# Down projection of a SwiGLU encoder block: 12 of 22 FFN pairs by seven block products, in two passes over the PSUM banks

## The chip, the cores and the metric

The kernel runs on one core of one Trainium2 chip. The metric is the device time of one execution in microseconds, where lower is better. Before the change three runs took 2675.44, 2680.14 and 2686.07 us, so the median is 2680.14 us.

## The reference

One encoder block is computed on 512 tokens of width 2048 in float32: token mixing (two attention branches, merged and projected), then a SwiGLU feed-forward network of width 5632, each with a residual and a LayerNorm. The change touches the end of the second part alone:

```python
h = modulate(layer_norm(x), shift2, scale2)
f = (jax.nn.silu(h @ w_ffn_gate[l]) * (h @ w_ffn_up[l])) @ w_ffn_down[l]
x = layer_norm_affine(DEEPNORM_ALPHA * x + gate2 * f, ln2_g[l], ln2_b[l])
```

## The kernel before

Every float32 operand of a matmul is split into a high part in the fp32r format and a low part (the remainder): ScalarE casts (line 97), VectorE subtracts (line 98, both inputs in SBUF). One block product is then three matmuls (`mm3`, lines 79 to 81).

The 5632 FFN features are 22 pairs of two 128-feature blocks. For pairs 2 to 21 the gate and up projections already use seven products in place of eight: a unit of work loads 512 KB of weights, `weight_sums` (line 1045) forms four sums of weight blocks on GpSimd (lines 1053 to 1055) and splits raw blocks and sums (ACT and DVE), and TensorE runs 42 matmuls with 256 columns. Four units make one projection of a pair. The hidden state of a pair (silu of gate times up, line 1133) goes to DRAM as one 512 KB transfer (`store_hid`, line 1010).

The down projection is plain. `down` (line 1166) goes over groups of four pairs. For each of four 512-column chunks it takes four PSUM banks (one for each 128-token tile) and for every pair of the group loads 256 rows by 512 columns of weights (512 KB), splits them (one cast, one subtraction of 128x1024) and runs 24 matmuls with 512 columns, as eight block products of a 128-feature block with a 128-token tile. `drain` (line 1150) then multiplies the four banks by the gate row and adds them to the residual in SBUF, on VectorE. Hidden states of the next group come back from DRAM (`load_hid`, line 1100: one transfer, one cast, one subtraction). The last two pairs go token tile by token tile, with weights that GpSimd has multiplied by the gate row (line 1203), so that the final LayerNorm can start early.

Staging: four tiles `raw` of 128x1024 take all loads, four tiles `wh` and four `wl` hold split weights. PSUM has eight banks: four with the tag s, two g, two t. The order of the instructions on each engine is not written by hand: it is fixed when the program is built. Each engine takes its own list in order, and so does each queue of DMA issues (SP issues the weight loads).

## Time and profile before

| what | value |
|---|---|
| median of three runs | 2680.14 us |
| the profiled execution: its own time | 2681.6 us |
| its span | 2679.8 us (1.8 us lie around it) |
| granted TensorE clock, mean | 0.987 of 2.4 GHz |
| busy: PE, DVE, ACT, POOL | 97%, 69%, 39%, 49% of the span |
| gate and up projections by products | about 1390 to 2185 us |
| down projection | about 2185 to 2668 us |

All instructions of one engine run in order, so a share of busy time says little by itself: what matters is whether TensorE finds its operands ready in a stage. A busy time of GpSimd or VectorE contains the time in which an instruction has been started and is held up, so the durations of equal instructions are compared below, the shortest with the longer ones.

### The profile page before, as it was taken

How to read it: one execution, taken by the hardware profiler on the slowest of the kernel's cores; microseconds unless marked ns; L12 is line 12 of the kernel's file. 1: busy time of each engine (PE TensorE's matmuls, PEld its weight loads, DVE VectorE, ACT ScalarE, POOL GpSimd, SP SyncE). 2: the span in 40 equal slices, each digit the busy share in tenths (PEclk: the TensorE clock that was granted, in tenths of full speed). 3: DMA queues.
4: the chain of work that ended last, by engine and by line, in shares of the span. 5: the costliest groups of instructions: out<-in, count | busy, mean ns of one | idle time of the engine just before them, and what ended most of it. 6: DMA issues, size and time to landing. Idle time of an engine off the chain costs nothing.

```text
span 2679.8 us, 40193 instructions
## 1 busy us (share of the span) xinstructions
PE 2601.6 (97%) x15563; PEld 2318.5 (87%) x15563; DVE 1846.5 (69%) x2178; ACT 1053.4 (39%) x1525; POOL 1303.1 (49%) x1093
## 2 busy tenths in 40 slices
PE   5999999999989999999899999999999999999998
...
DVE  8986688774678744577777777677677655445566
ACT  5542334332345533345644444444444432222321
POOL 4638788776764011011358767787776720000023
PEclk8999999999999999999999999999999999999999
...
GB/s 349 298 219 231 174 204 241 244 242 189 213 153 134 122 145 146 225 234 240 231 183 120 117 120 123 113 119 122 115 119 121 116 208 162 110 111 132 151 125 87
DMA packets 330799, 456.11 MB, mean 170 GB/s; under 512 B 19656, under 2 KB 208480, under 8 KB 330096
## 3 DMA queue, kind: packets, MB, share of 16 engines
...
## 4 chain that ended last, share of the span: by engine, by line
PE 46%; POOL 2%; issue 1%; DVE 1%; ACT 0%; POOLq 0%; DVEq 0%
PE ps_s L80 8%; PE ps_s L79 7%; PE ps_s L81 7%; PE ps_g L80 4%; PE ps_g L81 4%; PE ps_g L79 4%; PE ps_t L81 4%; PE ps_t L80 4%; PE ps_t L79 4%; POOL tt L1053 1%; POOL tt L1054 0%; POOL tt L1055 0%; DVE wl L98 0%; ACT wh L97 0%; DVE lr L1051 0%
## 5 line engine op out<-in xcount | busy, mean ns | idle before, releaser
L98 DVE TENSOR_TENSOR wl<-raw,wh 128x1024 fp32r<-128x1024 f32 (+2 forms) x342 | 452.1, 1326 | 328.3 <-ACT wh L97 324.9
L97 ACT CAST wh<-raw 128x1024 fp32r<-128x1024 f32 (+2 forms) x342 | 345.7, 1015 | 657.5 <-PE ps_s L81 262.9
L98 DVE TENSOR_TENSOR wl<-tt,wh 128x1024 fp32r<-128x1024 f32 x160 | 235.7, 1474 | 171.3 <-ACT wh L97 171.1
L1053 POOL TENSOR_TENSOR tt<-raw 128x512 f32<-128x512 f32 x160 | 249.3, 1559 | 184.3 <-DMA raw<-in_w_ffn_gate_dram 61.3
L232 POOL TENSOR_TENSOR acc<-acc,tmp 128x512 f32<-128x512 f32 (+1 forms) x214 | 295.6, 1381 | 74.9 <-ACT tmp L230 62.1
L97 ACT CAST wh<-tt 128x1024 fp32r<-128x1024 f32 x160 | 167.6, 1049 | 307.7 <-PE ps_s L80 136.8
L1051 DVE TENSOR_TENSOR lr<-raw,hr 128x768 fp32r<-128x768 f32 x160 | 217.8, 1362 | 42.6 <-ACT hr L1050 41.7
L1203 POOL TENSOR_TENSOR raw<-raw,gate 128x512 f32<-128x512 f32 x16 | 25.8, 1640 | 400.4 <-DMA raw<-in_w_ffn_down_dram 399.5
L228 POOL TENSOR_SCALAR tmp<-braw,csil 128x512 f32<-128x512 f32 x112 | 140.8, 1259 | 120.8 <-DMA braw<-in_w_ada_dram 117.6
L1050 ACT CAST hr<-raw 128x768 fp32r<-128x768 f32 x160 | 133.6, 835 | 150.8 <-PE ps_s L80 73.1
L1055 POOL TENSOR_TENSOR tt<-raw,tt 128x256 f32<-128x256 f32 x160 | 174.8, 1094 | 11.7
L1054 POOL TENSOR_TENSOR tt<-raw,tt 128x256 f32<-128x256 f32 x160 | 171.6, 1073 | 11.7
L79 PE MATMUL ps_g<-hTh,wh 128*128 128x512 f32 x384 | 153.4, 402 | 0.0
L80 PE MATMUL ps_g<-hTl,wh 128*128 128x512 f32 x384 | 151.2, 394 | 0.0
L81 PE MATMUL ps_g<-hTh,wl 128*128 128x512 f32 x384 | 151.2, 394 | 0.0
L222 DVE SCALAR_TENSOR_TENSOR acc<-braw,csil,acc 128x512 f32<-128x512 f32 x112 | 111.9, 1000 | 47.7 <-DMA braw<-in_w_ada_dram 46.8
L79 PE MATMUL ps_s<-wh,hTh 128*128 128x512 f32 (+1 forms) x384 | 138.1, 361 | 0.0
L80 PE MATMUL ps_s<-wl,hTh 128*128 128x512 f32 (+1 forms) x384 | 137.5, 358 | 0.0
L81 PE MATMUL ps_s<-sh,wl 128*128 128x256 f32 x480 | 135.9, 284 | 1.4 <-DVE wl L98 1.4
L81 PE MATMUL ps_s<-wh,hTl 128*128 128x512 f32 (+1 forms) x384 | 137.2, 358 | 0.0
L79 PE MATMUL ps_s<-sh,wh 128*128 128x256 f32 x480 | 135.1, 282 | 2.0 <-ACT wh L97 2.0
L80 PE MATMUL ps_s<-sl,wh 128*128 128x256 f32 x480 | 136.1, 284 | 0.0
...
## 6 DMA issues: line engine op xcount, KB each, us to landing
braw<-in_w_ada_dram SPq DMA_DIRECT2D x128, 512.0 KB, 4.2
...
```

The lines of the kernel that those rows point to most:

```text
L79: nc.tensor.matmul(ps, lhsT=ah, rhs=bh, start=start, stop=False)
L80: nc.tensor.matmul(ps, lhsT=ah, rhs=bl, start=False, stop=False)
L81: nc.tensor.matmul(ps, lhsT=al, rhs=bh, start=False, stop=stop)
L97: nc.scalar.copy(out=h[:, :n], in_=src)
L98: nc.vector.tensor_tensor(out=l[:, :n], in0=src, in1=h[:, :n], op=ALU.subtract)
L228: nc.gpsimd.tensor_scalar(out=dst[:, :n], in0=v[:, k, :], scalar1=col, scalar2=1.0, op0=ALU.mult, op1=ALU.mult)
L232: nc.gpsimd.tensor_tensor(out=acc2[:, :n], in0=acc2[:, :n], in1=dst[:, :n], op=ALU.add)
L1050: nc.scalar.copy(out=hr, in_=b[:, :, 1:4, :])
L1051: nc.vector.tensor_tensor(out=lr, in0=b[:, :, 1:4, :], in1=hr, op=ALU.subtract)
L1053: nc.gpsimd.tensor_tensor(out=t[:, :, 0:2, :], in0=b[:, :, 0:1, :].broadcast_to([P, 2, 2, P]), in1=b[:, :, 1:3, :], op=ALU.subtract)
L1054: nc.gpsimd.tensor_tensor(out=t[:, :, 2, :], in0=b[:, :, 2, :], in1=t[:, :, 0, :], op=ALU.subtract)
L1055: nc.gpsimd.tensor_tensor(out=t[:, :, 3, :], in0=b[:, :, 3, :], in1=t[:, :, 2, :], op=ALU.subtract)
```

## The change

For the 12 pairs 2 to 13 the down projection uses seven products in place of eight. The blocks of a pair are its two 128-feature blocks, two halves of the tokens and two halves of the output columns. Three of the products need one set of sums of hidden blocks and weight blocks, four need another, so that the 12 pairs are gone through twice (first pass, second pass), each time for both 1024-column halves c = 0 and c = 1 (in two 512-column pieces). The banks collect over all 12 pairs: six banks in the first pass, eight in the second.

- `hidden_sums` forms four sums of 128x256 on GpSimd when a pair of gate and up is done, and stores 7 blocks with six transfers from ACT's queue in place of one.
- `load_set` brings a set of hidden blocks back (three blocks for the first pass, four for the second), with a cast and a subtraction, into one of 12 ring tiles. Four of them (D) take the place of the pool of the gate and up stage.
- `weights1` (first pass, one unit of 18 matmuls): two transfers (512 and 256 KB), two subtractions of 128x512 on GpSimd, and two splits (1024 and 512 columns). `weights2` (second pass, one unit of 24 matmuls): four transfers of 256 KB, one subtraction of 128x1024 on GpSimd and one of 128x512 on VectorE, and two splits of 1024.
- `half_tile` alternates the four `raw` tiles with four new tiles `tp`, which lie in the pool on the right side, where the token sums sh and sl of the gate and up stage lay.
- The products' sums are collected in the x3 tiles, without the gate row. `convert` multiplies them by the gate row on GpSimd (128x1024) and adds the scaled residual on VectorE, four times for each half.
- The other eight pairs go through the plain `down` as before (now without the first-group case), the last two as before.

```diff
+    GROUPS = [[2, 3, 4, 5, 6, 7, 8, 9, 10, 11, 12, 13]]
+    PLAIN = [[0, 1, 14, 15], [16, 17, 18, 19]]
+    N_LAST = 2
+    by_sums = [g for grp in GROUPS for g in grp]
+    RING = [(a_pool, "Ah0"), (a_pool, "Al0"), (a_pool, "Ah1"), (a_pool, "Al1"),
+            (m0, "Mh0"), (m0, "Ml0"), (m0, "Mh1"), (m0, "Ml1")]
...
+    def half_tile():
+        place[1] += 1
+        if extra_tiles and place[1] % 2:
+            return extra_tiles[0].tile([P, 1024], F32, tag="tp", name="tp", bufs=4)
+        return raw_tile()
...
+    def load_set(arr, g, n):
+
+        v = half_tile()[:, :n * 256].rearrange("p (b n) -> p b n", b=n)
+        nc.sync.dma_start(out=v, in_=arr[g])
+        tl = ring_tile((n, g))
+        nc.scalar.copy(out=tl[:, 0:n, 0:256], in_=v)
+        nc.vector.tensor_tensor(out=tl[:, 0:n, 256:512], in0=v, in1=tl[:, 0:n, 0:256], op=ALU.subtract)
+        return tl
...
+    def hidden_sums(g, eg, e):
+
+        nc.gpsimd.tensor_tensor(out=e[:, 0], in0=eg[:, 1], in1=eg[:, 2], op=ALU.add)
+        nc.gpsimd.tensor_tensor(out=e[:, 1], in0=e[:, 0], in1=eg[:, 3], op=ALU.subtract)
+        nc.gpsimd.tensor_tensor(out=e[:, 2], in0=eg[:, 1], in1=eg[:, 3], op=ALU.subtract)
+        nc.gpsimd.tensor_tensor(out=e[:, 3], in0=eg[:, 0], in1=e[:, 1], op=ALU.subtract)
+        nc.scalar.dma_start(out=set1_d[g][:, 0:2, :], in_=e[:, 0:2])
+        nc.scalar.dma_start(out=set1_d[g][:, 2, :], in_=eg[:, 3])
+        for b, (t, k) in enumerate(((eg, 0), (e, 2), (eg, 2), (e, 3))):
+            nc.scalar.dma_start(out=set2_d[g][:, b, :], in_=t[:, k])
...
-        store_hid(g, eg)
...
+        if g in by_sums:
+            hidden_sums(g, eg, eu)
+        else:
+            store_hid(g, eg)
...
+    dr = push("dr", "left")
+    vacant += range(len(RING), len(RING) + 4)
+    RING += [(dr, f"D{i}") for i in range(4)]
...
+    def weights1(g, c):
+        a, b = half_tile(), half_tile()
+        av, bv = a.rearrange("p (b n) -> p b n", b=2), b[:, :512]
+        nc.sync.dma_start(out=av, in_=w_rows(g, 0, c))
+        nc.sync.dma_start(out=bv, in_=w_rows(g, 1, c)[:, 1, :])
+        nc.gpsimd.tensor_tensor(out=av[:, 1], in0=av[:, 1], in1=av[:, 0], op=ALU.subtract)
+        nc.gpsimd.tensor_tensor(out=bv, in0=bv, in1=av[:, 1], op=ALU.subtract)
+        ah, al = split(a, 1024)
+        bh, bl = split(bv, 512)
+        return ((2, (ah[:, :512], al[:, :512])), (1, (bh[:, :512], bl[:, :512])), (0, (ah[:, 512:], al[:, 512:])))
+
+    def weights2(g, c):
+        a, b = half_tile(), half_tile()
+        av, bv = a.rearrange("p (b n) -> p b n", b=2), b.rearrange("p (b n) -> p b n", b=2)
+        for j in range(2):
+            nc.sync.dma_start(out=av[:, j], in_=w_rows(g, 1, c)[:, 1 - j, :])
+            nc.sync.dma_start(out=bv[:, j], in_=w_rows(g, 0, c)[:, 1 - j, :])
+        nc.gpsimd.tensor_tensor(out=bv, in0=bv, in1=av, op=ALU.subtract)
+        nc.vector.tensor_tensor(out=bv[:, 1], in0=bv[:, 0], in1=bv[:, 1], op=ALU.subtract)
+        ah, al = split(a, 1024)
+        bh, bl = split(b, 1024)
+        return ((3, (ah[:, :512], al[:, :512])), (0, (ah[:, 512:], al[:, 512:])), (1, (bh[:, :512], bl[:, :512])),
+                (2, (bh[:, 512:], bl[:, 512:])))
...
+    def products(pairs, sets, weights, c, step):
+        bk = None
+        for u, g in enumerate(pairs):
+            ws = weights(g, c)
+            if bk is None:
+                bk = [dbank() for _ in range(2 * len(ws))]
+            step(u, False)
+            for j, (b, w) in enumerate(ws):
+                for i in range(2):
+                    mm3(bk[2 * j + i], block(sets[g], b, i), w, u == 0, u == len(pairs) - 1)
+            step(u, True)
...
+    def convert(c, ts=range(NT)):
+        for t in ts:
+            zv = quad(x2[t], c)
+            xc = half_tile().rearrange("p (b n) -> p b n", b=2)
+            nc.sync.dma_start(out=xc, in_=quad(x2_d[t], c))
+            nc.gpsimd.tensor_tensor(out=zv, in0=zv, in1=quad(gate2, c), op=ALU.mult)
+            nc.vector.scalar_tensor_tensor(out=zv, in0=xc, scalar=ALPHA, in1=zv, op0=ALU.mult, op1=ALU.add)
...
+                    vacate((3, pairs[u]))
+                if done:
+                    tick((lambda g=pairs[u]: need2(g)) if c == 1 else None)
+            bk = products(pairs, set1, weights1, c, step)
...
+        for c in range(2):
+            def step(u, done):
+                if done and c == 1:
+                    vacate((4, pairs[u]))
+                if done:
+                    tick(following.pop(0) if following and c == 1 else None)
+                if done and c == 1 and final and u % 2 and u // 2 < NT:
+                    convert(0, [u // 2])
+            bk = products(pairs, set2, weights2, c, step)
+            for i in range(2):
+                add(nc.vector, z(0, 1, i, c), bk[i])
+            for i in range(2):
+                add(nc.vector, z(0, 0, i, c), bk[2 + i])
+            for i in range(2):
+                add(nc.vector, z(1, 0, i, c), bk[4 + i])
+                add(nc.vector, z(1, 1, i, c), bk[4 + i])
+            for i in range(2):
+                add(nc.vector, z(1, 0, i, c), bk[6 + i])
...
+    if PLAIN:
+        convert(1)
+        for grp in PLAIN:
+            queue = down(grp, (0, 2, 1, 3), queue)
```

How the order of the instructions moves, at three places (names carry a buffer's number; the rows of the changed kernel have its own line numbers, some 190 lines further down at the end).

First VectorE. Before, in the first group of the down projection: the subtraction of the last gate and up pair, then for each unit one split of 128x1024 (line 98), and drains.

```order
L1133 TENSOR_TENSOR eg_21845<-eg_21845,eu_22324 128x1024
L98 TENSOR_TENSOR wl_22450<-raw_22447,wh_22449 128x1024
L98 TENSOR_TENSOR wl_22496<-raw_22493,wh_22495 128x1024
L98 TENSOR_TENSOR wl_22526<-raw_22523,wh_22525 128x1024
L98 TENSOR_TENSOR wl_22556<-raw_22553,wh_22555 128x1024
L1153 TENSOR_TENSOR dtmp_22477<-ps_s_22348,gate2_22347 128x512
L1153 TENSOR_TENSOR dtmp_22480<-ps_s_22349,gate2_22347 128x512
L1156 SCALAR_TENSOR_TENSOR x3_0_22340<-x3_0_22340,dtmp_22477 128x512
L1156 SCALAR_TENSOR_TENSOR x3_1_22341<-x3_1_22341,dtmp_22480 128x512
L1153 TENSOR_TENSOR dtmp_22483<-ps_s_22350,gate2_22347 128x512
L1153 TENSOR_TENSOR dtmp_22486<-ps_s_22351,gate2_22347 128x512
L1156 SCALAR_TENSOR_TENSOR x3_2_22342<-x3_2_22342,dtmp_22483 128x512
```

Now, in the second half (c = 1) of the second pass, each unit has three rows: line 1212 (the weight difference) and two of line 98. Between them stand line 1333 (a plain pair's hidden state) and line 1254 (`convert`).

```order
L1333 TENSOR_TENSOR Al1_24177<-tp_24175,Al1_24177 128x1024
L98 TENSOR_TENSOR wl_24144<-tp_24135,wh_24143 128x1024
L98 TENSOR_TENSOR wl_24148<-raw_24136,wh_24147 128x1024
L1254 SCALAR_TENSOR_TENSOR x3_3_22452<-tp_24225,x3_3_22452 128x2x512
L1333 TENSOR_TENSOR Mh0_24222<-raw_24220,Mh0_24222 128x1024
L1212 TENSOR_TENSOR tp_24181<-tp_24181 128x512
L98 TENSOR_TENSOR wl_24189<-raw_24180,wh_24188 128x1024
L98 TENSOR_TENSOR wl_24193<-tp_24181,wh_24192 128x1024
L1212 TENSOR_TENSOR tp_24230<-tp_24230 128x512
L1333 TENSOR_TENSOR Ml0_24271<-raw_24269,Ml0_24271 128x1024
L98 TENSOR_TENSOR wl_24238<-raw_24229,wh_24237 128x1024
L98 TENSOR_TENSOR wl_24242<-tp_24230,wh_24241 128x1024
```

One row for a unit has become three to five, all with both inputs in SBUF. In the whole pass half, nine rows of line 1333 and four of line 1254 stand ahead of the last unit's split. In the first pass it is seven loads of three blocks (line 1126) for c = 0 and nine of four blocks for c = 1, and three more stand in c = 0 of the second pass.

Second GpSimd. Before, from the end of gate and up (lines 1053 to 1055) its next rows are those of the last two pairs, line 1203:

```order
L1055 TENSOR_TENSOR tt_22208<-raw_22202,tt_22208 128x2x128
L1053 TENSOR_TENSOR tt_22268<-raw_22262 128x2x256
L1054 TENSOR_TENSOR tt_22268<-raw_22262,tt_22268 128x2x128
L1055 TENSOR_TENSOR tt_22268<-raw_22262,tt_22268 128x2x128
L1203 TENSOR_TENSOR raw_24776<-raw_24776,gate2_22347 128x512 x2
L1203 TENSOR_TENSOR raw_24784<-raw_24784,gate2_22347 128x512 x2
```

Now the first pass stands there with two rows for each unit, here at the turn from c = 0 to c = 1:

```order
L1199 TENSOR_TENSOR tp_22904<-tp_22904 128x512
L1200 TENSOR_TENSOR raw_22905<-raw_22905,tp_22904 128x512
L1199 TENSOR_TENSOR tp_22942<-tp_22942 128x512
L1200 TENSOR_TENSOR raw_22943<-raw_22943,tp_22942 128x512
L1199 TENSOR_TENSOR tp_22974<-tp_22974 128x512
L1200 TENSOR_TENSOR raw_22975<-raw_22975,tp_22974 128x512
L1199 TENSOR_TENSOR tp_23006<-tp_23006 128x512
L1200 TENSOR_TENSOR raw_23007<-raw_23007,tp_23006 128x512
```

GpSimd, which had no row in 20 pairs of the down projection, has 24 x 2 rows of 128x512 and 24 of 128x1024 there, and eight of `convert`, four of them after the fourth unit of the second pass's last half.

Third SP's queue at the turn from gate and up to down, with what each issue waits for. Now (tp is the new staging tile, set_d the stored sets):

```order
L1197 DMA raw<-in_w_ffn_down_dram 128x2x512 [waits DMAHW6_49,DVE_49]
L1123 DMA raw<-set_d 128x768 [waits DMAHW3_49,DVE_49]
L1198 DMA raw<-in_w_ffn_down_dram 128x512 [waits DMAHW7_49,DVE_49,Pool_49]
L1197 DMA raw<-in_w_ffn_down_dram 128x2x512 [waits DMAHW4_49,DMAHW0_49,DVE_49]
L1123 DMA raw<-set_d 128x768 [waits DMAHW2_49,DVE_49]
L1198 DMA raw<-in_w_ffn_down_dram 128x512 [waits DMAHW5_49,DVE_49]
L1198 DMA tp<-in_w_ffn_down_dram 128x512 [waits PE_49]
L1197 DMA tp<-in_w_ffn_down_dram 128x2x512 [waits DMAHW1_49]
```

Before, all issues of this place wrote `raw` and waited for its readers alone:

```order
L1103 DMA raw<-hid_d 128x1024 [waits DMAHW7_49,DVE_49]
L91 DMA raw<-in_w_ffn_down_dram 128x2x512 [waits DMAHW2_49,DVE_49]
L91 DMA raw<-in_w_ffn_down_dram 128x2x512 [waits DMAHW3_49,DVE_49,Pool_49]
L91 DMA raw<-in_w_ffn_down_dram 128x2x512 [waits DMAHW4_49,DMAHW0_49,DVE_49]
L91 DMA raw<-in_w_ffn_down_dram 128x2x512 [waits DMAHW5_49,DVE_49]
```

The first issue into `tp` (the second weight block of the first unit) waits for TensorE, which reads sh and sl until the end of the last gate and up pair, and all later issues stand behind it.

## Rows read from the trace of the kernel before

**Rows 1.** It is the profile's first page: the span and the busy time of each engine, and the span in 40 equal slices with the busy tenths of PE, DVE, ACT and POOL and the granted TensorE clock in tenths.

```profile
span 2679.8 us, 40193 instructions
...
PE 2601.6 (97%) x15563; PEld 2318.5 (87%) x15563; DVE 1846.5 (69%) x2178; ACT 1053.4 (39%) x1525; POOL 1303.1 (49%) x1093
...
PE   5999999999989999999899999999999999999998
...
DVE  8986688774678744577777777677677655445566
ACT  5542334332345533345644444444444432222321
POOL 4638788776764011011358767787776720000023
PEclk8999999999999999999999999999999999999999
```

**Rows 2.** It is the busy time by stretch: start and end, length, then busy us and instructions of PE, PEld, DVE, ACT and POOL, the granted clock (1.00 is 2.4 GHz), the busy share of the DMA engines and GB/s. The first three stretches lie in the gate and up projections (the third is the most crowded one there), the last two in the down projection (2190 to 2212 is its start).

```profile
1420.00:2100.00 680.00, 679.11 (x5667) 678.88 (x5666) 488.73 (x425) 282.19 (x323) 510.91 (x412) 1.00 0.37 119
1440.00:1480.00 40.00, 39.11 (x326) 38.88 (x325) 30.05 (x27) 17.66 (x21) 37.02 (x28) 1.00 0.42 132
1500.00:1700.00 200.00, 200.00 (x1671) 200.00 (x1671) 144.01 (x126) 83.42 (x95) 143.21 (x120) 1.00 0.38 119
2190.00:2212.00 22.00, 22.00 (x99) 18.20 (x98) 7.33 (x9) 4.26 (x5) 0.00 (x0) 1.00 0.94 317
2190.00:2640.00 450.00, 450.00 (x1987) 372.73 (x1986) 238.97 (x288) 108.57 (x112) 26.64 (x18) 1.00 0.42 136
```

**Rows 3.** It is the view of one tile, tt (the gate and up weight sums), from 1500 to 2100 us: count, then minimum, median and maximum duration in ns.

```profile
L1054 POOL TENSOR_TENSOR tt<-raw,tt x120: 733/742/1607, 1499.7 to 2099.6; 128x256 f32<-128x256 f32 x120
L97 ACT CAST wh<-tt x120: 1047/1048/1058, 1500.4 to 2099.4; 128x1024 fp32r<-128x1024 f32 x120
...
L98 DVE TENSOR_TENSOR wl<-tt,wh x119: 1214/1505/1934, 1501.5 to 2095.4; 128x1024 fp32r<-128x1024 f32 x119
L1053 POOL TENSOR_TENSOR tt<-raw x119: 1274/1405/2093, 1504.1 to 2097.5; 128x512 f32<-128x512 f32 x119
```

**Rows 4.** It is the same view of the tile lr (the low part of raw gate and up blocks), from 1500 to 2100 us.

```profile
L1051 DVE TENSOR_TENSOR lr<-raw,hr x120: 943/1015/2095, 1498.4 to 2097.4; 128x768 fp32r<-128x768 f32 x120
```

**Rows 5.** It is the same view of the tile raw (where weights and hidden states land) in the down projection, from 2190 to 2680 us, with the DMA issues of SP (SPq) and, in the last row, the time from issue to landing.

```profile
L91 SPq DMA_DIRECT2D raw<-in_w_ffn_down_dram x82: 367/368/384, 2189.9 to 2596.0; - x82
L97 ACT CAST wh<-raw x77: 1044/1055/1057, 2192.0 to 2603.5; 128x1024 fp32r<-128x1024 f32 x77
L98 DVE TENSOR_TENSOR wl<-raw,wh x77: 1212/1224/2208, 2193.6 to 2607.5; 128x1024 fp32r<-128x1024 f32 x77
...
L1203 POOL TENSOR_TENSOR raw<-raw,gate x16: 1287/1474/2279, 2532.4 to 2601.5; 128x512 f32<-128x512 f32 x16
...
L1205 ACT CAST Ah<-raw x8: 621/622/627, 2533.8 to 2559.1; 128x512 fp32r<-128x512 f32 x8
L1206 DVE TENSOR_TENSOR Al<-raw,Ah x8: 674/903/1579, 2534.4 to 2560.7; 128x512 fp32r<-128x512 f32 x8
...
DMA to landing us min/median/max: 3.6/3.7/5.7
```

**Rows 6.** It is VectorE in order of time, from 1632 to 1640 us: start in us, duration in us, engine, line, operation, out<-in and shapes, and in brackets idle time before it.

```profile
1632.71 1.75 DVE L98 TENSOR_TENSOR wl<-tt,wh 128x1024 fp32r<-128x1024 f32 x1
1634.39 1.49 DVE L1051 TENSOR_TENSOR lr<-raw,hr 128x768 fp32r<-128x768 f32 x1
```

**Rows 7.** It is GpSimd over the same time, with the same columns.

```profile
1631.79 1.59 POOL L1054 TENSOR_TENSOR tt<-raw,tt 128x256 f32<-128x256 f32 x1
1633.46 1.60 POOL L1055 TENSOR_TENSOR tt<-raw,tt 128x256 f32<-128x256 f32 x1
1635.03 2.01 POOL L1053 TENSOR_TENSOR tt<-raw 128x512 f32<-128x512 f32 x1
```

**Rows 8.** It is the instructions of GpSimd by line from 1440 to 1480 us: count, busy us, mean ns, and idle time before them.

```profile
L1054 POOL TENSOR_TENSOR tt<-raw,tt 128x256 f32<-128x256 f32 x10 | 14.3, 1433 | 0.6
L1055 POOL TENSOR_TENSOR tt<-raw,tt 128x256 f32<-128x256 f32 x10 | 12.2, 1230 | 0.6
L1053 POOL TENSOR_TENSOR tt<-raw 128x512 f32<-128x512 f32 x8 | 12.0, 1498 | 1.7 <-DVE wl L98 1.7
```

**Rows 9.** It is the same for VectorE from 1440 to 1480 us.

```profile
L98 DVE TENSOR_TENSOR wl<-tt,wh 128x1024 fp32r<-128x1024 f32 x9 | 13.1, 1455 | 11.3 <-ACT wh L97 11.2
L1051 DVE TENSOR_TENSOR lr<-raw,hr 128x768 fp32r<-128x768 f32 x9 | 11.8, 1311 | 0.0
L1133 DVE TENSOR_TENSOR eg<-eg,eu 128x1024 f32<-128x1024 f32 x1 | 1.8, 1765 | 0.0
...
L1085 DVE TENSOR_TENSOR eg<-ps_s,eg 128x512 f32<-128x512 f32 x1 | 0.7, 691 | 0.0
```

**Rows 10.** It is VectorE by line in the down projection, from 2190 to 2480 us.

```profile
L1158 DVE TENSOR_TENSOR x<-x,dtmp 128x512 f32<-128x512 f32 x36 | 23.3, 685 | 0.0
L1153 DVE TENSOR_TENSOR dtmp<-ps_s,gate 128x512 f32<-128x512 f32 x28 | 18.2, 684 | 0.4
L1156 DVE SCALAR_TENSOR_TENSOR x<-x,dtmp 128x512 f32<-128x512 f32 x16 | 10.4, 686 | 0.0
```

243 lines of the change are left out of this document (155 added, 88 removed).

## The prediction

> **What bounds the kernel now.** I read the first page first: TensorE is busy 97% of the span, at full clock in all but the first slice [rows 1]. A busy TensorE may still run at a poor pace, so the second view is the stretches [rows 2]. In the down projection 1987 matmuls of 512 columns start in 450 us: 450 / 1987 = 226.5 ns each, and TensorE is never idle. In gate and up it is 680 / 5667 = 120 ns for 256 columns, with 0.9 us lost in 680. So TensorE bounds both stages, and a matmul taken away is worth its pace, as long as what feeds TensorE keeps up.
>
> The third view is what feeds it. In gate and up GpSimd is busy 511 and VectorE 489 of 680 us [rows 2], but equal instructions of theirs differ by up to a factor of two: GpSimd's 128x256 takes 0.73 to 1.61 us, its 128x512 1.27 to 2.09, VectorE's subtraction of 128x1024 1.21 to 1.93, that of 128x768 0.94 to 2.10 [rows 3, 4]. In the down projection, where GpSimd is idle, that subtraction has a median of 1.22 [rows 5]. The two time lines say why [rows 6, 7]. GpSimd's 128x256 ends at 1633.38; VectorE's subtraction, begun at 1632.71, ends 1.08 later, at 1634.46. GpSimd's next, begun at 1633.46, ends 0.60 after that, at 1635.06; VectorE's 128x768, begun at 1634.39, ends 0.82 after that; and GpSimd's 128x512 ends 1.16 after that. While one runs, the other stands still. I call 1.08, 0.82, 1.16 and 0.60 us the holds of these shapes. The ban holds for VectorE operations with two SBUF inputs: one that reads a bank keeps its 0.69 us in the most crowded stretch [rows 9].
>
> How tightly can holds be packed? From 1440 to 1480 us GpSimd ran 8 of 128x512 and 20 of 128x256, VectorE 10 of 1024 columns and 9 of 768 [rows 8, 9]: 8 x 1.16 + 20 x 0.60 + 10 x 1.08 + 9 x 0.82 = 39.5 us, some 37.5 without an operation cut at either end, so 0.94 to 0.99 of 40, and there TensorE lost 0.9 us [rows 2]. Over 1500 to 1700 (120 GpSimd operations, five pairs of 40 us) it is 40 x (1.16 + 2 x 0.60) + 40 x (1.08 + 0.82) + 5 x 1.08 = 176 us of 200, 0.88, and TensorE lost nothing [rows 2]. I take 0.95 as the limit.
>
> The Trainium skill has this as a rule that speaks against the change (SBUF — State Buffer, Who interferes with whom): a VectorE instruction with two SBUF inputs and a GpSimd instruction that reads SBUF exclude each other for the whole instruction. The trace agrees that one stands still, but not on the whole length: after the other's end 1.08 us are left of an instruction that takes 1.21 alone, and 1.16 of 1.27. Counted by whole instructions (1.22, 0.94 and 0.68 us on VectorE, 1.27 and 2.35 on GpSimd) the four half passes would lose 52 us in place of 38.5 as an estimate, and the sum would be 2708.
>
> **What is taken away.** Each of 12 pairs loses 96 - 84 = 12 matmuls, 144 in all, and TensorE's list is shorter by just that: 144 x 0.2265 = **-32.6 us**. The Trainium skill (TensorE: Matmul & The Clock Gate, Back-to-back issue gap) gives 216 ns for an isolated matmul of 512 columns and 131 in a sustained stream with weight loads. As estimates, by the one the gain would be 31.1 us, by the other 18.9. The 226.5 ns measured here decide against both, so neither gets a chance of its own.
>
> **What is added in the down projection.** A unit of the first pass has 18 matmuls, 4.08 us of TensorE; one of the second 24, 5.44. Two holds have no row. For GpSimd's 128x1024 I go on from 0.60 and 1.16 in a line: 1.16 + 2 x 0.56 = 2.28; its bounds are 1.16 (no dearer than 512 columns) and 2.32 (twice that). For VectorE's 128x512, 0.82 - 0.26 = 0.56, between 0 and its unblocked 0.68 [rows 10]. `convert`'s VectorE operation of 1024 columns I take as a subtraction, 1.08, since the two kinds cost the same 0.68 to 0.69 at 512 [rows 10]. Then one unit holds
>
> - first pass: 2 x 1.16 + 1.08 + 0.56 = 3.96 us;
> - second pass: 2.28 + 0.56 + 2 x 1.08 = 5.00 us.
>
> The loads come on top. By half passes (12 units each):
>
> - first, c = 0: 47.5 + 7 x 0.82 = 53.3, less 3.4 done before the stage (1.16 + 1.08 + 1.16 for what fits into `raw`) = 49.9; at 0.95 52.5 against 48.9 us of TensorE: +3.6.
> - first, c = 1: 47.5 + 9 x 1.08 = 57.2; 60.3 against 48.9: +11.3.
> - second, c = 0: 60.0 + 3 x 1.08 = 63.2; 66.6 against 65.2: +1.3.
> - second, c = 1: 60.0 + 9 x 1.08 + 4 x (2.28 + 1.08) = 83.2; 87.5 against 65.2: +22.3.
>
> Together **+38.5 us**. Split weights are two units ahead at most (four `wh`, two to a unit), so little can be saved up from one half to the next. Packed without any gap it is 1.0 + 8.3 + 0 + 18.0 = 27.3; packed to 0.88, 7.8 + 16.1 + 6.6 + 29.3 = 59.8.
>
> **The turn from gate and up.** The first load into `tp` waits for TensorE's last sh and sl product, and SP's queue, all weight loads, stands behind it. What follows is one issue and landing 0.37 + 3.7, GpSimd 1.16, a cast 0.62, a subtraction 0.68: 6.5 us [rows 5]. TensorE meanwhile has the 12 matmuls of the unit's other block, 2.7 us. I take **+4**, between 0 (the pool lets go earlier) and 6.5.
>
> **Smaller terms.** In gate and up `hidden_sums` adds 4 x 0.60 = 2.4 us of holds to a pair of 336 x 0.12 = 40.3: 0.88 becomes 0.94, just under the limit. VectorE's queue is not blocked by it, since the sums stand some units later in GpSimd's list than their input. I take 0.25 us for a pair, **+3**; bounds 0, and (0.94 / 0.92 - 1) x 40.3 = 0.9 for each, 10. The six stores instead of one are issued by ACT, 39% busy [rows 1]. Draining the banks costs VectorE 4, 4, 10 and 10 bank reads of 0.68 [rows 10]; they ban nothing, and the banks that are needed first were finished half a unit earlier. I take **+2** for the turns, between 0 and 7 (one turn's ten reads). Bringing in the residual (`convert`, c = 1), plain pairs and the last pairs run where VectorE is busy 239 of 450 us [rows 2]: nothing; without that cover four conversions cost 4 x 3.36 = 13. Clock: full throughout the stage before; gaps of 1 to 2 us in a unit could lower it, but then TensorE is waiting anyway.
>
> **Sum:** -32.6 + 38.5 + 4 + 3 + 2 = +14.9 on the profiled execution's 2681.6, so 2696.5. That execution is 1.5 above the median of the runs (2680.1), so I give **2695**. A measurement of this kernel can tell about 0.5% (13.4 us) from no change: the forecast lies just beyond.
>
> **Rivals.**
>
> 1. *Packed holds, no change.* The holds of both engines follow each other without a gap, since both have work queued. Then 27.3 in place of 38.5, 2 for the turn and nothing else: -32.6 + 27.3 + 2 = -3, **2677**. For it: the stretch with 0.94 to 0.99 [rows 8, 9]. Against it: that stretch is short, and a VectorE operation that follows its own kind takes 1.22, not 1.08 [rows 5].
> 2. *The holds fit under TensorE, faster.* If GpSimd's subtraction of whole rows held much less than the gate and up sums do, every unit would be ready in time: -32.6 + 4 + 2 = -27, **2654**. Its place is the first pass with c = 1. It decides when 24 GpSimd operations and VectorE's 12 x 1.64 + 9.7 = 29.4 us fit into 0.95 x 48.9 = 46.5: from 0.71 us for 512 columns downward. For it: no row has the large plain shape. Against it: the plain 128x512 of line 1203 takes at least 1.29 unblocked, as line 1053 does (1.27) [rows 3, 5].
> 3. *The staging tiles, slower still.* With a load a unit of the first pass takes three of eight tiles. A tile's round is 0.37 + 3.7 landing, 2 x 1.16 GpSimd, 1.06 cast, 1.22 subtraction [rows 5], and one hold of waiting on each side, 2.2: 10.9 us. At 8 / 3 = 2.7 units that is 4.1 us a unit, no more than TensorE's own. But 1.31 MB in a unit of 5.0 us is 262 GB/s, where 317 kept the DMA engines 94% busy [rows 2]. If landing takes twice as long, the round is 14.6 us, 5.5 a unit, 0.5 more on 16 units, and late data opens gaps between holds: with packing at 0.90, 55.4 + 63.6 + 70.2 + 92.4 - 228.2 = 53.4, the sum becomes -32.6 + 53.4 + 4 + 3 + 2 + 8 = +38, **2718**.
>
> **How the numbers follow.** Forecast case 0.48, packed holds 0.22, fitting holds 0.14, staging tiles 0.16. The forecast case spreads over packing 0.92 to 0.97, some 2684 to 2712, with two fifths of it within 0.5%. So slower by over 0.5%: 0.58 x 0.48 + 0.16 = 0.44; within 0.5%: 0.22 + 0.20 less 0.02 for the low end of rival 1 = 0.40; faster: 0.14 + 0.02 = 0.16. The range, 2662 to 2726, takes in packing without gaps and at 0.88 with the other terms as chosen (-32.6 + 59.8 + 9 = +36) and a part of the bounds of the smaller terms; it leaves out most of rival 2 and the upper end of rival 3, under 0.2.
>
> **What would show it.** TensorE starts exactly 144 fewer matmuls, still at 226 ns where fed. The first pass with c = 1 lasts about 60 us and the last half of the second about 87, with VectorE and GpSimd together in use without a break and their equal shapes longer than alone; the second pass with c = 0 about 66. GpSimd's 128x1024 takes at least 2.3 us unblocked. At the turn TensorE stands for some 4 us. In the plain pairs nothing is lost. I am wrong if the four half passes take about 228 us (rival 2), if GpSimd's shape is far from 2.3, or if TensorE waits mainly for landings.

## The result and the profile after

The changed kernel takes 2709.4 us (median of four runs, 2707.6 to 2720.7), the kernel before 2678.3 (four runs): ratio 1.012, 95% interval 1.0101 to 1.014. So it is slower by some 31 us. All differences of whole kernels here are under 2%; one is called slower or faster where the interval of its ratio leaves out 1. The forecast was 2695, about 15 slower. The profiled execution takes 2710.6 us with a span of 2708.8, 29.0 longer than that of before.

The first page of the changed kernel, as [rows 1]:

```profile
span 2708.8 us, 40614 instructions
...
PE 2587.2 (96%) x15419; PEld 2292.5 (85%) x15419; DVE 1964.6 (73%) x2194; ACT 1101.0 (41%) x1585; POOL 1556.7 (57%) x1213
...
PE   6999999999989999999899999999999989888998
...
POOL 4638778776744011031279998899767658555003
```

TensorE starts 15563 - 15419 = 144 fewer matmuls, as promised, and is yet less busy in a longer span: slices 33 and 35 to 37 show gaps where before there were none. The second view is the busy time by stretch, with the columns of [rows 2]. The first six stretches go from the first matmul of a half pass to the first of the next: first pass c = 0 and 1, second pass c = 0 and 1, first and second group of plain pairs. Then come a short piece at the turn, and the start of the pairs with sums in gate and up.

```profile
2189.35:2253.31 63.96, 53.84 (x218) 40.52 (x217) 56.46 (x37) 26.43 (x34) 47.69 (x27) 0.95 0.75 245
2253.31:2308.72 55.41, 51.53 (x217) 39.76 (x216) 55.41 (x38) 30.93 (x37) 42.10 (x22) 1.00 0.82 266
2308.72:2384.99 76.27, 68.40 (x289) 54.50 (x288) 55.60 (x48) 31.17 (x33) 38.64 (x14) 0.98 0.61 200
2384.99:2467.60 82.61, 69.31 (x288) 53.12 (x289) 74.95 (x56) 30.01 (x31) 40.19 (x14) 1.00 0.70 230
2467.60:2567.03 99.43, 91.61 (x385) 74.80 (x384) 70.67 (x65) 24.74 (x24) 31.05 (x11) 0.95 0.41 132
2567.03:2654.07 87.04, 87.04 (x385) 72.07 (x384) 42.46 (x51) 16.77 (x16) 2.41 (x1) 1.00 0.27 85
2198.00:2201.00 3.00, 2.95 (x7) 1.80 (x8) 0.71 (x2) 1.32 (x2) 2.54 (x3) 0.50 1.01 344
1420.00:1480.00 60.00, 56.60 (x466) 55.79 (x465) 43.16 (x37) 22.73 (x28) 53.62 (x45) 1.00 0.41 128
```

At 0.2265 us for each of 216, 216, 288, 288 and 384 matmuls TensorE needs 48.9, 48.9, 65.2, 65.2 and 87.0 us. So 15.0, 6.5, 11.0, 17.4 and **12.4** us were lost in the first five stretches, 62.4 together; the second plain group lost nothing. From the first matmul of the down projection to the last of the kernel it is 508.0 us, before 478.5: -32.6 + 62.4 = +29.8, measured +29.5. Gate and up took 3.2 us more, and everything ahead of it 3.7 less in this execution (the 7000th matmul starts at 1411.8 us, before at 1415.5), which makes the 29.0 of the spans.

What TensorE waited for says the same by cause. It is the view of waits (instruction waiting, what released it, us in all, times, longest), for the first pass with c = 0 (two rows), the second with c = 0 (three) and with c = 1 (four), and the first plain group (two):

```profile
PE ps_s L79 <- ACT wh L97: 5.5, 1, 5.5
PE ps_s L80 <- DVE wl L98: 4.5, 7, 1.2
...
PE ps_g L80 <- DVE wl L98: 3.4, 2, 2.7
PE ps_s L79 <- DVE x L1282: 2.2, 1, 2.2
...
PE ps_g L79 <- DVE x L1246: 1.0, 1, 1.0
...
PE ps_g L80 <- DVE wl L98: 7.8, 7, 1.9
PE ps_s L80 <- DVE wl L98: 2.7, 2, 1.5
PE ps_s L79 <- DVE x L1246: 1.9, 2, 1.6
PE ps_g L79 <- DVE x L1246: 1.7, 2, 1.0
...
PE ps_g L80 <- DVE wl L98: 4.1, 1, 4.1
PE ps_g L79 <- DVE x L1246: 3.7, 1, 3.7
```

VectorE's low part (line 98) ends most waits of the passes. Two kinds of wait are larger than forecast: one of 5.5 us for the very first weights, and those for VectorE's drains of a bank (lines 1246 and 1282). Two rows of the views of one tile bear on the terms: the landing of the issues into tp from 2185 to 2200 us, and GpSimd's 128x1024 (minimum, median and maximum in ns).

```profile
DMA to landing us min/median/max: 6.0/7.3/8.5
```

```profile
L1211 POOL TENSOR_TENSOR raw<-raw,tp x16: 2399/2927/3489, 2307.3 to 2451.1; 128x1024 f32<-128x1024 f32 x16
```

The first is far from the 3.7 us of [rows 5]; the second is 2.40 where nothing holds it up.

In the plain group TensorE waits twice. The first wait (3.7 us, to 2472.86) is for a drain. Ahead of it in VectorE's list stands the hidden state of a plain pair (line 1333), and VectorE is idle until ScalarE has cast that, which waits for its landing (the issue is at 2461.93, 7.0 us before the cast). The time lines show it (start, duration, then as in [rows 6]):

```profile
2470.03 2.17 DVE L1333 TENSOR_TENSOR D<-raw,D 128x1024 fp32r<-128x1024 f32 x1 [5.01 <-ACT D L1332]
2472.12 0.68 DVE L1246 TENSOR_TENSOR x<-ps_g,x 128x512 f32<-128x512 f32 x1
...
2468.95 1.05 ACT L1332 CAST D<-raw 128x1024 fp32r<-128x1024 f32 x1 [5.79 <-DMA raw<-hid_d]
```

So this wait is for a landing, passed on by the order of VectorE's list, and no hold. What stood ahead of the second wait (4.1 us, to 2494.80) is seen in VectorE's and GpSimd's time lines from 2480 us:

```profile
2479.80 1.63 DVE L98 TENSOR_TENSOR wl<-raw,wh 128x1024 fp32r<-128x1024 f32 x1
2481.35 3.41 DVE L1254 SCALAR_TENSOR_TENSOR x<-raw,x 128x1024 f32<-128x1024 f32 x1
2484.68 0.68 DVE L1246 TENSOR_TENSOR x<-ps_s,x 128x512 f32<-128x512 f32 x1
2485.28 2.83 DVE L1254 SCALAR_TENSOR_TENSOR x<-tp,x 128x1024 f32<-128x1024 f32 x1
2488.04 3.43 DVE L1254 SCALAR_TENSOR_TENSOR x<-raw,x 128x1024 f32<-128x1024 f32 x1
2491.39 6.67 DVE L98 TENSOR_TENSOR wl<-raw,wh 128x1024 fp32r<-128x1024 f32 x2
```

```profile
2480.31 3.37 POOL L1362 TENSOR_TENSOR tp<-tp,gate 128x1024 f32<-128x1024 f32 x1
2483.63 3.40 POOL L1253 TENSOR_TENSOR x<-x,gate 128x1024 f32<-128x1024 f32 x1
2486.99 3.40 POOL L1362 TENSOR_TENSOR raw<-raw,gate 128x1024 f32<-128x1024 f32 x1
2490.35 3.32 POOL L1253 TENSOR_TENSOR x<-x,gate 128x1024 f32<-128x1024 f32 x1
```

Here the two engines go strictly by turns. Read as in the prediction, from the end of the other engine's operation to its own end, VectorE's 1024 columns hold for 1.08 us (from 2483.68 to 2484.76) and GpSimd's for 2.2 to 2.3 (to 2487.03). GpSimd's operations start 3.3 to 3.4 us apart, VectorE's take 2.8 to 3.4 us in place of 1.21, and the weights that TensorE needs next (line 98, from 2491.39) stand behind three conversions (line 1254).

### The profile page after: what moved, and what is told of

The parts are those of the page before. It is cut to its first block, busy times and chain, and to the rows that moved or that the text cites. A ratio compares the mean times of both kernels' runs of the same rounds, so it can differ in the third digit from the quotient of the medians.

```text
span 2708.8 us, 40614 instructions
## 1 busy us (share of the span) xinstructions
PE 2587.2 (96%) x15419; PEld 2292.5 (85%) x15419; DVE 1964.6 (73%) x2194; ACT 1101.0 (41%) x1585; POOL 1556.7 (57%) x1213
## 5 line engine op out<-in xcount | busy, mean ns | idle before, releaser
L98 DVE TENSOR_TENSOR wl<-raw,wh 128x1024 fp32r<-128x1024 f32 (+2 forms) x342 | 490.1, 1438 | 230.4 <-ACT wh L97 228.9
L97 ACT CAST wh<-raw 128x1024 fp32r<-128x1024 f32 (+2 forms) x342 | 339.3, 995 | 584.2 <-PE ps_s L81 238.6
L98 DVE TENSOR_TENSOR wl<-tt,wh 128x1024 fp32r<-128x1024 f32 x160 | 227.1, 1422 | 191.4 <-ACT wh L97 187.8
L1055 POOL TENSOR_TENSOR tt<-raw 128x512 f32<-128x512 f32 x160 | 239.2, 1496 | 106.7 <-DMA raw<-in_w_ffn_up_dram 53.7
L1053 DVE TENSOR_TENSOR lr<-raw,hr 128x768 fp32r<-128x768 f32 x160 | 211.4, 1322 | 42.2 <-ACT hr L1052 41.5
L1056 POOL TENSOR_TENSOR tt<-raw,tt 128x256 f32<-128x256 f32 x160 | 202.7, 1268 | 10.7
L230 POOL TENSOR_SCALAR tmp<-braw,csil 128x512 f32<-128x512 f32 x112 | 133.9, 1198 | 118.9 <-DMA braw<-in_w_ada_dram 115.5
L1057 POOL TENSOR_TENSOR tt<-raw,tt 128x256 f32<-128x256 f32 x160 | 192.5, 1204 | 11.6
L80 PE MATMUL ps_g<-sl,wh 128*128 128x256 f32 x480 | 135.8, 283 | 0.0
```

The costliest lines, as they stand in the source:

```text
L80: nc.tensor.matmul(ps, lhsT=ah, rhs=bl, start=False, stop=False)
L97: nc.scalar.copy(out=h[:, :n], in_=src)
L98: nc.vector.tensor_tensor(out=l[:, :n], in0=src, in1=h[:, :n], op=ALU.subtract)
L230: nc.gpsimd.tensor_scalar(out=dst[:, :n], in0=v[:, k, :], scalar1=col, scalar2=1.0, op0=ALU.mult, op1=ALU.mult)
L1053: nc.vector.tensor_tensor(out=lr, in0=b[:, :, 1:4, :], in1=hr, op=ALU.subtract)
L1055: nc.gpsimd.tensor_tensor(out=t[:, :, 0:2, :], in0=b[:, :, 0:1, :].broadcast_to([P, 2, 2, P]), in1=b[:, :, 1:3, :], op=ALU.subtract)
```

## Experiments

The theory is the prediction's: VectorE's operations with two SBUF inputs and GpSimd's exclude each other, and the sum of their holds paces the half passes. Its rivals are late transfers, and VectorE's own list (its length, or the order in it). For each kernel the half passes are read off stretches as above, with the same columns.

Each stretch comes from one execution, and kernels whose edits do not touch it show how far it scatters. In the changed kernel, spread, conv_vec and plain_vec the first pass takes 61.4 to 64.7 us with c = 0 and 54.8 to 58.6 with c = 1, the second with c = 0 76.3 to 80.1. In the changed kernel, gate_late and turn_raw the second with c = 1 takes 81.4 to 82.6, and in these three, no_sub and vec_sub the first plain group takes 98.0 to 99.6. A smaller difference than that shows nothing.

**no_sub**: without GpSimd's three subtractions of weights, so that the weight sums are left out.

```diff
-        nc.gpsimd.tensor_tensor(out=av[:, 1], in0=av[:, 1], in1=av[:, 0], op=ALU.subtract)
-        nc.gpsimd.tensor_tensor(out=bv, in0=bv, in1=av[:, 1], op=ALU.subtract)
...
-        nc.gpsimd.tensor_tensor(out=bv, in0=bv, in1=av, op=ALU.subtract)
```

> The changed kernel without the three GpSimd subtractions of weights1 and weights2 (the weight sums are left out; transfers, casts, VectorE's subtractions and all matmuls stay). Holds theory: what TensorE lost in the four half passes beside the turn and the drains (about 6 us in the first pass with c = 0, 6.5 with c = 1, 3 and 13 in the second) comes back, since GpSimd then works there only on the four conversions: the first pass with c = 1 falls from 55.4 us to 49 or 50, the second with c = 1 from 82.6 to about 69, the whole from 2709 to about 2680 (2674 to 2686). Landing theory (late transfers and staging tiles): the same transfers through the same tiles, so the half passes stay within 2 us each and the time stays at 2705 to 2712.

Measured: 2679.2 us, as the holds theory expected, ratio to the kernel before 1.0003 (0.9994 to 1.0012). The four half passes and the first plain group:

```profile
2186.30:2243.03 56.73, 51.04 (x218) 41.43 (x217) 33.59 (x39) 25.89 (x35) 0.00 (x0) 0.94 0.82 277
2243.03:2292.27 49.24, 49.24 (x217) 40.50 (x216) 36.09 (x40) 30.21 (x36) 0.00 (x0) 1.00 0.85 283
2292.27:2361.84 69.57, 67.43 (x290) 54.97 (x288) 41.27 (x45) 30.36 (x32) 0.00 (x0) 0.98 0.66 219
2361.84:2434.80 72.96, 68.66 (x288) 54.48 (x289) 61.16 (x56) 31.83 (x32) 14.51 (x6) 0.98 0.79 274
2434.80:2532.78 97.98, 90.05 (x385) 73.40 (x384) 70.95 (x65) 23.86 (x24) 29.23 (x10) 0.97 0.41 129
```

The first pass with c = 1 is fed without a gap (49.24), though its transfers come at 283 GB/s in place of 266. The four half passes are 29.7 us shorter with the same transfers through the same tiles: the landing theory falls. The second with c = 1 comes to 73.0, where about 69 was expected. VectorE's busy time in that half pass falls from 55.4 to 36.1 us though it lost no operation: the difference was standing still. The plain group's loss stays (98.0 us).

**vec_sub**: the three subtractions on VectorE, in those lines; the last of the three is shown.

```diff
-        nc.gpsimd.tensor_tensor(out=bv, in0=bv, in1=av, op=ALU.subtract)
+        nc.vector.tensor_tensor(out=bv, in0=bv, in1=av, op=ALU.subtract)
```

> The same three subtractions, moved from GpSimd to VectorE. Holds theory: VectorE's 512-column subtraction takes 0.59 us from start to start, its 1024-column one 1.13, in place of GpSimd's holds of 1.16 and 2.24. One unit of the first pass is then 3 x 0.59 + 1.13 = 2.9 us of VectorE against 4.08 of TensorE, of the second 0.59 + 3 x 1.13 = 4.0 against 5.44; with loads of 1.13 a unit 4.0 and 5.1, still under TensorE. The first pass with c = 1 takes 49 to 51 us (55.4), the second with c = 1 loses only what the conversions and drains cost, 72 to 75 us (82.6); whole 2681 to 2688. Landing theory: no change, 2705 to 2712. Third theory, that VectorE's own list is the limit (busy 100% of the first pass with c = 1 already): the added work makes it slower, 2715 or more.

Measured: 2685.7 us, as expected, ratio 1.0024 (1.0014 to 1.0035). The first pass, the second with c = 1 and the first plain group:

```profile
2188.99:2247.83 58.84, 52.26 (x218) 41.82 (x217) 50.29 (x67) 27.20 (x35) 0.00 (x0) 0.94 0.83 272
2247.83:2297.81 49.98, 49.34 (x218) 40.47 (x216) 47.26 (x57) 29.11 (x36) 0.00 (x0) 1.00 0.87 291
2366.24:2443.84 77.60, 70.79 (x289) 55.45 (x289) 73.15 (x69) 30.58 (x31) 13.10 (x5) 0.96 0.75 251
2443.84:2542.57 98.73, 91.32 (x386) 74.61 (x385) 70.38 (x62) 24.64 (x24) 32.45 (x11) 0.95 0.42 134
```

VectorE does 19 operations more in the first pass with c = 1 (57 in place of 38), is busy 8 us less, and the half pass takes 50.0 us in place of 55.4. VectorE's length was not the limit. The second pass with c = 1 (77.6) is longer than the 72 to 75 expected; GpSimd's conversions are still in it, but that they cost this was not tested.

Both edits also take a slow step out of each unit's way to TensorE: GpSimd's 128x1024 takes 2.40 us alone, VectorE's 1.21. The first pass with c = 1 speaks for the holds all the same. In the changed kernel VectorE is busy there for all of 55.41 us, with operations stretched by GpSimd's; the same list takes it 36.1 in no_sub. GpSimd itself waited for landings in the changed kernel (51.6 us in all ahead of line 1211 with its output in raw). Since the same transfers come faster in no_sub and vec_sub, these waits look like an effect of tiles that are let go late; no run shows that by itself.

**spread**: the conversions behind the passes, tied behind earlier instructions (the main part of the edit).

```diff
-                if done and c == 1 and final and u % 2 and u // 2 < NT:
-                    convert(0, [u // 2])
...
+                if residual and n < 2:
+                    with tc.issue_after(last['low']), tc.issue_after(last['drain']), tc.issue_after(last['sub']):
+                        convert(n, [u])
```

> The changed kernel with the conversions moved behind the two passes: those of c = 0 into the first chunk of the first plain group, those of c = 1 into its second chunk, each queued behind the drains on VectorE and behind a unit's low-part subtraction. Holds theory: the second pass with c = 1 has 12 x 5.00 + 9 x 1.08 = 69.7 us of holds in place of 83.2, so it takes 73 to 77 us in place of 82.6; in the plain pairs VectorE and GpSimd have room, so the 12.4 us lost there fall to 6 or less; whole 2690 to 2698. Landing theory: the conversions' transfers only move, the half pass stays at 82 and the whole at 2705 to 2712. If GpSimd and VectorE cannot take eight conversions in 44 us beside the plain weights, the loss moves into the plain pairs and the whole stays.

Measured: 2708.2 us, ratio 1.0103 (1.0088 to 1.0118); the second pass with c = 1 takes 83.9 us, the first plain group 95.6. The expectation of the holds theory missed, and the numbers are those expected of late transfers. The trace shows why the edit proves little: it moved VectorE's half of a conversion, but GpSimd's four multiplications ran as soon as its last subtraction of weights was done:

```profile
2446.53 11.75 POOL L1253 TENSOR_TENSOR x<-x,gate 128x1024 f32<-128x1024 f32 x4
```

From then on VectorE's weights of the last units went by turns with them (3.4 us each). And that last subtraction (line 1211, at 2443.13) had itself waited 3.9 us for a landing. So the run does not part the two theories.

**gate_late** and **turn_raw** look at the turn from gate and up. The first makes the gate row's transfers wait for a drain and issues them in the second pass (the move is not shown), the second takes the first eight tiles from raw:

```diff
+                        nc.scalar.copy(out=gate2[:, cc * 512:cc * 512 + 1], in_=z(0, 0, 0, 0)[:, 0:1])
                         nc.scalar.dma_start(out=gate2[:, cs], in_=rows_d[1][cs].partition_broadcast(P))
```

```diff
-        if extra_tiles and place[1] % 2:
+        if extra_tiles and place[1] % 2 and place[1] > 8:
```

> The changed kernel with the four transfers of the gate row (256 KB each into SBUF) made to wait for the first pass's first drain, so that they no longer run at the turn. If they are what makes the first weights land late there (6.4 us after their issue in place of 3.7), TensorE's wait of 5.7 us becomes about 3 and the 7.8 us lost up to 2202 become about 5: whole 2705 to 2708. If the wait is for the pool that holds the token sums and for the chain GpSimd, cast, subtraction behind it, the turn stays at 5.7 us and the whole at 2709.

> The changed kernel with the first eight tiles of half_tile taken from raw, so that the first two units' weights do not lie in tp, whose pool becomes free only with TensorE's last product of the gate and up stage. If the turn is lost to that release (issue at 2189.3, landing 6.4 us later, then GpSimd, cast and subtraction), TensorE's wait of 5.7 us falls to 2 us or less, the first pass with c = 0 from 64.0 to about 59, the whole to 2703 to 2706. If the turn is lost to the holds of GpSimd and VectorE alone, the first wait moves to the second unit and the half pass stays at 63 to 64 us.

Measured: gate_late 2709.9 us, ratio 1.0101 (1.0083 to 1.0119); turn_raw 2707.5, ratio 1.0099 (1.0086 to 1.0112). As wholes both missed (2705 to 2708 and 2703 to 2706 expected), the turn itself did as expected. In the first the long gap between two matmuls there falls from 5.9 to 2.9 us, in the second the longest in the first 19 us is 1.2; the first 21 matmuls, which lose 7.8 us in the changed kernel, lose 4.8 and 0.0. The stage takes 503.5 and 503.7 us in place of 508.0; the 4.5 us of gate_late do not show in its median, and its stage starts at 2194.8 us in its profile, 2189.35 in that of the changed kernel. The half passes of turn_raw (first pass, then second with c = 0):

```profile
2184.26:2240.91 56.65, 51.47 (x219) 39.89 (x218) 53.88 (x36) 25.18 (x32) 42.48 (x24) 1.00 0.80 266
2240.91:2298.91 58.00, 52.20 (x217) 39.61 (x216) 57.73 (x40) 31.04 (x38) 41.29 (x23) 1.00 0.78 255
2298.91:2376.67 77.76, 68.68 (x289) 54.33 (x288) 55.05 (x47) 31.35 (x32) 36.93 (x15) 0.98 0.60 198
```

So the turn was lost to the release of tp and the long landing behind it, the gate row's transfers being 3.0 of the 7.8 us, and 7.3 us come back in the first half pass. The next two are 2.6 and 1.5 us longer, which lies within the scatter; whether holds take back a part of what is won ahead of them stays open.

**conv_vec** and **plain_vec** look at the plain group: the conversions' multiplications on VectorE (the first two lines); and in plain_vec those of load_last too (the last two).

```diff
-            nc.gpsimd.tensor_tensor(out=zv, in0=zv, in1=quad(gate2, c), op=ALU.mult)
+            nc.vector.tensor_tensor(out=zv, in0=zv, in1=quad(gate2, c), op=ALU.mult)
...
-            nc.gpsimd.tensor_tensor(out=v, in0=v, in1=gate2[:, cc * 512:(cc + 1) * 512].unsqueeze(1).broadcast_to([P, 2, 512]), op=ALU.mult)
+            nc.vector.tensor_tensor(out=v, in0=v, in1=gate2[:, cc * 512:(cc + 1) * 512].unsqueeze(1).broadcast_to([P, 2, 512]), op=ALU.mult)
```

> The changed kernel with the multiplications by the gate row in convert (eight of 128x1024) moved from GpSimd to VectorE. Holds theory: a conversion then takes 2 x 1.13 = 2.26 us of VectorE in place of 3.37 in turns with GpSimd, and GpSimd's three early multiplications of the last pairs' weights alone are left at the start of the plain pairs. The second pass with c = 1 falls from 82.6 to about 78 us, the 12.4 us lost in the first plain group to 7 or 8; whole 2698 to 2703. Theory of VectorE's order (what counts is that conversions and drains stand ahead of the next weights in its list): two operations stand there in place of one, nothing is won, 2706 to 2712.

> The changed kernel with the conversions' multiplications and those of the last pairs' weights (load_last) on VectorE, in their old places, so that in the plain pairs no GpSimd instruction runs before the final LayerNorm; the weight sums stay on GpSimd. Theory that the loss in the plain pairs is holds of GpSimd (VectorE's 1024-column operations take 3.4 us in turns with GpSimd's there): the 12.4 us lost in the first plain group (8.5 with only the conversions moved) fall to 3 to 5, whole 2697 to 2703. Theory of VectorE's order (conversions stand ahead of the next weights whoever multiplies): 8 us or more stay, 2706 to 2712. The half passes before it change by the conversions alone, 1 to 3 us.

Measured: conv_vec 2710.9 us, ratio 1.0116 (1.0101 to 1.0131); plain_vec 2705.4, ratio 1.0099 (1.0084 to 1.0114). The first plain group of the one and of the other:

```profile
2475.07:2570.57 95.50, 88.91 (x385) 73.17 (x384) 69.42 (x66) 24.64 (x24) 17.37 (x7) 0.96 0.42 136
```

```profile
2471.96:2563.95 91.99, 89.15 (x386) 73.06 (x384) 65.13 (x75) 23.94 (x24) 0.00 (x0) 0.98 0.45 142
```

The loss there goes 12.4, 8.5, 5.0 us as GpSimd leaves. But the 7.4 us that come back are not holds alone, since VectorE's order moved as well: in both kernels the first drains now stand ahead of the hidden state of line 1333, and the wait of 3.7 us for a drain is gone. In plain_vec:

```profile
2470.88 0.68 DVE L1246 TENSOR_TENSOR x<-ps_g,x 128x512 f32<-128x512 f32 x1
...
2476.74 1.21 DVE L1333 TENSOR_TENSOR D<-raw,D 128x1024 fp32r<-128x1024 f32 x1
```

How the 7.4 us divide between holds and order, these runs do not show. The second pass with c = 1, where conv_vec was to bring about 78 us, takes 81.7 and 81.6, within the scatter: there the conversions cost no less on VectorE. As wholes both missed (2698 to 2703 and 2697 to 2703 expected). In conv_vec the second pass with c = 0 took 80.1 us in place of 76.3, which its edit does not explain and which is the upper end of the scatter.

**all_vec**: the edits of vec_sub, plain_vec, spread, gate_late and turn_raw together (with no GpSimd instruction left to be queued, one tie of spread goes, which is shown):

```diff
-                    with tc.issue_after(last['low']), tc.issue_after(last['drain']), tc.issue_after(last['sub']):
+                    with tc.issue_after(last['low']), tc.issue_after(last['drain']):
```

> Everything together: no GpSimd instruction in the down projection before the final LayerNorm (the weight sums, the conversions and the last pairs' multiplications run on VectorE), the first eight tiles from raw, the gate row fetched later, the conversions behind the passes. Holds theory: the four half passes need 2.9 + 1.13 and 4.0 + 1.13 us of VectorE a unit where TensorE needs 4.08 and 5.44; left are about 3 us at the turn, 2 in the rest of the first half pass, 1, 3 and 4 in the others and 4 in the plain pairs, 17 against the 32.6 taken away, and 3 us in gate and up: whole 2660 to 2672, so faster than the kernel before by some 0.5%. If VectorE's list alone is too long (12 units, loads, 16 conversion operations), the loss of the second pass with c = 1 and of the first plain group stays at 10 us each and the whole comes to 2678 to 2690.

Measured: **2663.7 us**, ratio 0.994 (0.9927 to 0.9952): faster than the kernel before, as the holds theory expected. Its half passes and first plain group:

```profile
2189.06:2240.94 51.88, 49.57 (x219) 40.40 (x217) 47.91 (x64) 26.30 (x38) 0.00 (x0) 1.00 0.82 275
2240.94:2294.02 53.08, 50.31 (x218) 40.11 (x216) 46.75 (x58) 28.89 (x35) 0.00 (x0) 1.00 0.87 294
2294.02:2364.29 70.27, 66.30 (x290) 53.68 (x288) 59.43 (x62) 32.11 (x33) 0.00 (x0) 1.00 0.67 219
2364.29:2431.32 67.03, 65.87 (x289) 53.90 (x289) 61.89 (x64) 33.51 (x33) 0.00 (x0) 1.00 0.76 257
2431.32:2519.94 88.62, 87.74 (x384) 72.00 (x385) 72.08 (x81) 21.70 (x21) 0.00 (x0) 1.00 0.54 168
```

Left are 3.0 + 4.2 + 5.0 + 1.8 + 1.6 = 15.6 us of the 62.4, the clock stays full, and the stage takes 461.2 us in place of 478.5.

**sums_vec** and **more_pairs** go on from all_vec: hidden_sums on VectorE (the first of its four lines is shown); and a second group of six pairs in two passes, with its sums into x3 on VectorE (the groups are shown).

```diff
-        nc.gpsimd.tensor_tensor(out=e[:, 0], in0=eg[:, 1], in1=eg[:, 2], op=ALU.add)
+        nc.vector.tensor_tensor(out=e[:, 0], in0=eg[:, 1], in1=eg[:, 2], op=ALU.add)
```

```diff
-    GROUPS = [[2, 3, 4, 5, 6, 7, 8, 9, 10, 11, 12, 13]]
-    PLAIN = [[0, 1, 14, 15], [16, 17, 18, 19]]
+    GROUPS = [[2, 3, 4, 5, 6, 7, 8, 9, 10, 11, 12, 13], [14, 15, 16, 17, 18, 19]]
+    PLAIN = [[0, 1]]
```

> The version with no GpSimd instruction in the down projection (2664 us), and in gate and up the four sums of hidden_sums on VectorE too. Holds theory: four of 128x256 hold GpSimd's 0.60 us each and VectorE's about 0.3, so the 2 to 3 us that gate and up lose in the first pairs with sums fall to about 1: 1000 matmuls from the 7000th on take 121 to 121.6 us (before 121.1, changed 124.3), whole 2660 to 2664. If VectorE's list is the tighter one there, the loss grows to 4 us or more.

> The version with no GpSimd instruction in the down projection, with six more pairs (14 to 19) by seven products, as a second group of two passes over the banks; two plain pairs are left. It takes away 6 x 12 x 0.2265 = 16.3 us of TensorE. Each half pass of six units is 24.5 or 32.6 us of TensorE and has to drain six or eight banks: 12 or 10 operations of 0.6 us more on VectorE, whose units take 2.9 and 4.0 us with loads of 1.13 on top. If the drains hide as in the first group (2 to 3 us lost at each of four turns), whole 2654 to 2660; if VectorE's list becomes the limit, with 7 us more in 24.5 twice, the gain is lost again: 2662 to 2672.

Measured: sums_vec 2663.0 us, ratio 0.9945 (0.9928 to 0.9961), no different from all_vec; its 1000 matmuls from the 7000th on take 123.7 us, within what the kernels with the sums on GpSimd show (122.4 to 124.3), so the price of the sums did not fall as expected. more_pairs 2675.0 us, ratio 0.9983 (0.9971 to 0.9994), slower than all_vec by 11: beside the 16.3 us taken away, the four short half passes lose 4.1, 4.2, 8.3 and 2.4 us and the two plain pairs, which now carry all conversions, 11.5. Both expectations of its gain were too good.

## Why the prediction came out as it did

The mechanism and the direction held; the loss was two fifths larger than forecast: 62.4 us in the down projection in place of 44.5.

- **Taken away, -32.6.** Right: 144 fewer, still 87.04 / 384 = 0.2267 us each where TensorE is fed.
- **Holds of the half passes, +38.5.** Nearly right as a sum. The four half passes lost 49.9 us. Off that go 7.8 at the turn (the first 21 matmuls, up to 2202 us) and 6.8 of waits for drains (2.2 and 1.0 in the second pass with c = 0, 1.9 and 1.7 with c = 1); 35.3 are left. The first pass and its turn were to take 116.8 us and took 119.4; the second with its drains 156.1 and 158.9. GpSimd's 128x1024, which had no row, was taken as 2.28 and holds for 2.2 to 2.3 in the lines above; alone it takes 2.40. no_sub and vec_sub show that it is GpSimd's subtractions.
- **The half passes one by one** were wrong, and their errors nearly cancel. Less the turn and the drains they lost 7.2, 6.5, 7.8 and 13.8 us where 3.6, 11.3, 1.3 and 22.3 were forecast. The three lengths given as signs missed with them: 55.4 us for about 60, 76.3 for about 66, 82.6 for about 87. The sentence that failed is that "little can be saved up from one half to the next". GpSimd has 27, 22, 14 and 14 operations in the four stretches, where the program has 24, 24, 12 and 16 (one that crosses an end is counted twice): work ran ahead into the half before. An estimate by the prediction's holds of the operations that end in each stretch gives 57, 54, 70 and 75 us, where 50, 57, 63 and 83 were counted, with nearly the same sum. By it the holds fill 0.94 to 1.01 of each half's time less the turn and the drains, 0.97 of all four, near the 0.95 taken.
- The Trainium skill's rule that the whole instruction is exclusive (SBUF — State Buffer, SBUF: two separate sides) would have given 52 us here, as an estimate. That counts no gap between the operations, while the 38.5 beside it does; packed to 0.95 as that is, it would be 67. The 35.3 left for the half passes speak for the shorter holds, and so do the turns of 3.3 to 3.4 us, where 2.40 and 1.21 would make 3.6.
- **The turn, +4.** Too low, and over its bound of 6.5: 7.8, of which 5.7 are the wait and 2.1 the low clock behind it. The step that failed is the landing of 3.7 us [rows 5]: at the turn the issues into tp land 6.0 to 8.5 us later, beside the gate row's 1 MB and the weight loads, with the DMA engines full (share 1.01 from 2198 to 2201). turn_raw takes the loss of the first 21 matmuls away.
- **hidden_sums, +3.** Right in size: 1000 matmuls from the 7000th on take 124.3 us, before 121.1. But it is lost in the first pairs with sums alone, not 0.25 us in each pair: from the 8000th to the end of gate and up both kernels take 653.3. The experiments with the same sums took 122.4 to 124.3, so the price is 1.4 to 3.2.
- **Drains, +2.** Mis-sized: 6.8 in the half passes. I priced the bank reads at 0.68 each and took VectorE's list ahead of them as free, while operations of 2.8 to 3.4 us stood in it (one of 3.41 at 2311.95, ahead of the drain of line 1282 at 2317.03).
- **Plain pairs, nothing.** This is the step that failed: 12.4. The text had the right price, "without that cover four conversions cost 4 x 3.36 = 13", and then took VectorE's busy 239 of 450 us as the cover. That is an average. The order packs the conversions, the first multiplications of the last pairs' weights and nine drains into the first 32 us of the group. What came in place of nothing are two waits, 7.8 us together: one for a hidden state that landed late ahead of the drains in VectorE's list, one behind three conversions in turns with GpSimd. The low clock behind them makes most of the rest. plain_vec gives 7.4 of the 12.4 back with GpSimd gone and the order moved, all_vec nearly all by moving the conversions too.
- **Clock, nothing.** Wrong: in or behind gaps of 5.9, 2.6, 4.1 and 4.5 us between two matmuls the granted clock fell to 0.50 (1.2 GHz), and 30 matmuls took 0.427 us in place of 0.2265: 6.0 us, part of the losses above. They started one behind the other, so TensorE was fed and not waiting; whether later waits would have taken up the 6.0 us at full clock, no run shows. Behind the gaps of 1.0 to 2.3 us in this stage, which the prediction feared, the clock stayed full.

With 17.8 us for these (12.4 in the plain group; 2.6 and 2.8 in the passes, which is within the scatter) the stage's forecast of +11.9 becomes the +29.5 measured.

The rivals: packed holds (2677) had 27.3 for the 35.3 measured, further off than the forecast's 38.5, and the turn, the drains and the plain pairs, counted there with 2, lost 27.0. Fitting holds (2654) needed 0.71 us for GpSimd's 512 columns, which take 1.26 at least (line 1200), and half passes of 228 us in all, which took 278. The staging tiles (2718) came nearest in time, but not by their mechanism: no_sub and vec_sub run the same transfers through the same eight tiles faster. Late landings did cost something, at the turn and at the start of the plain group, where it did not place them.
